# A hybrid attention and recurrence layer: which engine copies the second head's weights, how the recurrence's output is stored, and when the decay column is projected

## The chip, the core and the metric

The kernel runs on one core of a Trainium2 chip. The metric is the device time of one execution in microseconds (us); the time of a kernel is the median over its runs. The engines are PE (matrix products), DVE (VectorE), ACT (ScalarE), POOL (GpSimd) and SP, which here only issues DMA transfers. A measurement of this kernel tells a difference of about 0.2%, some 3.6 us, from no change.

## The reference, cut

One layer over 1024 tokens with 16 meta tokens ahead of them (1040 rows), width 1024. Its input projection feeds two branches; everything is fp32.

```python
xn = rms_norm(h, norm_mix[layer])
proj = xn @ w_in[layer]
q_sb, k_sb, v_sb, rw, gate_sb, gate_rw = jnp.split(proj, in_splits, axis=-1)
# branch 1: stick-breaking attention, 8 heads of 64, causal (s < t), z = q.k / 8
#   A[t,s] = sigmoid(z_ts) * prod_{s<j<t} (1 - sigmoid(z_tj));  y_sb = A @ v
# branch 2: RWKV-7 recurrence, 8 heads of 64
rw = token_shift(rw, mu_rw[layer])
r, kr, vr, w_lo, a_lo, g_lo = jnp.split(rw, rw_splits, axis=-1)
w_log = -jax.nn.softplus(-(w0[layer] + jnp.tanh(w_lo) @ w_up[layer])) - 0.5
decay = jnp.exp(-jnp.exp(w_log))
a = jax.nn.sigmoid(a0[layer] + a_lo @ a_up[layer])
g = jax.nn.sigmoid(g_lo) @ g_up[layer]
# S_t = S_{t-1} diag(decay_t) + (S_{t-1} (-kk_t)) (kk_t * a_t)^T + v_t k_t^T ;  y_t = S_t r_t
y_rw = rwkv7_recurrence(r_h, split_heads(decay, RW_HEADS), k_h, v_h, kk, a_h)
y_rw = (group_norm_heads(y_rw, ...) + bonus) * g
merged = sigmoid(gate_sb) * (y_sb @ w_sb_out) + sigmoid(gate_rw) * (y_rw @ w_rw_out)
h = h + merged @ w_out[layer]
hn = rms_norm(h, norm_ffn[layer])
gate_ffn, up_ffn = jnp.split(hn @ w_ffn_in[layer], [FFN_HIDDEN], axis=-1)
h = h + (jax.nn.silu(gate_ffn) * up_ffn) @ w_ffn_out[layer]
return rms_norm(h, norm_final)[:, N_META:N_META + s]
```

## The kernel before, in words

**Split numbers.** Every fp32 operand of a large product is split into a rounded part "hi" (a copy on ACT, L146 or L155) and the rounded rest "lo" (a subtraction on DVE, L147; for weights on DVE or, where the flag LOP[0] is set, on POOL, L156). A product is then three matmuls: hi by hi, lo by hi, hi by lo (L254 to L256 in the projection).

**Start.** The input is normalised and transposed, and the first column of the input projection starts while that goes on: `wa`, the column of 128 weights that holds the low-rank decay and learning-rate inputs (`win[0]`, L284). A column is 8 k-steps of 3 matmuls over three pieces of 348, 346 and 346 tokens: 72 matmuls. Then `g_cols` (from L590) projects the output gate's two low-rank columns (`win[1]` and the 32-row `wg2`), applies the sigmoid (L606), splits the results (L146, L147, and L611) and multiplies them by the gate's second factor: eight banks `psg` of 512 tokens, four matmuls each (L621 to L624), copied by DVE (L625) and stored as `d_G`.

**Recurrence.** It works in chunks of 64 tokens. A unit is 8 or 9 chunks of one pair of heads; there are 8 units. Three generators (`stage1`, `stage2a`, `stage2b`) make a unit's chunk matrices, solve them, and run the chain of states (`Sbd`, L533 to L538). At the end of a unit `stage2b` transposes its output (L558), scales it on ACT (L560), adds the bonus (L561), multiplies by the gate (L564) and stores it as fp32 in `d_y` (L565, on SP). PE's order is written by a loop that gives every step a time by hand and fills with the remaining projection columns (`sb_col`: attention's q, k, v and the branch gates). Those columns leave through a ring of two tiles named `stage`, stored by POOL's DMA queue. The other engines' order is the framework scheduler's.

**Attention.** Per pair of heads and block i of 128 queries, and per head h: `psz` = q.k (L788, L789, mask L791), two sigmoids on ACT (`ub` L792, `be` L793), a running product over `ub` on DVE (L795), its product with `be` on DVE (L796), transposes of the weights on PE into banks `psaT` of up to four blocks (L804), copies of those banks to `aT`: the first 16 rows by ACT (L807), the rest of a first bank by DVE and later banks by ACT (L809, L810), then `pso` = weights by v for both heads (L814) and a split of that (`ysh`, `ysl`). While attention waits, PE is filled with the recurrent branch's product `psbr` (L836 to L838): its input is loaded from `d_y` in eight pieces `yv` (L825) and split there into `yrh` (ACT, L146) and `yrl` (DVE, L147).

**Behind that** come the attention branch's product, the output projection, the FFN's first product in two halves of seven block products each (L957 to L959), the second product (`psfo`, L1119 to L1121, its tiles in the pool `w5`), and the last norm.

Of the kernel before, what the change touches and what calls it, by code (L numbers as in the profile page):

```python
# [10 lines left out]
F32 = mybir.dt.float32  # L11
F32R = mybir.dt.float32r
BF16 = mybir.dt.bfloat16
AF = mybir.ActivationFunctionType
# [5 lines left out]
S = 1024  # L20
# [74 lines left out]
def _build(nc, tc, I, out, dbg, es):  # L95
# [5 lines left out]
    V, A, G, T, SY = nc.vector, nc.scalar, nc.gpsimd, nc.tensor, nc.sync  # L101
# [37 lines left out]
    d_k = dr.tile([2, 4, 128, L], F32, name="d_k")  # L139
    d_v = dr.tile([4, 128, L], F32, name="d_v")  # L140
    d_g = dr.tile([16, 128, S], F32, name="d_g")
    d_y = dr.tile([4, 128, S], F32, name="d_y")
    d_G = dr.tile([4, 128, S], F32, name="d_G")

    def split(hi, lo, src):
        A.copy(hi, src)  # L146
        V.tensor_tensor(lo, src, hi.bitcast(F32), op=ALU.subtract)  # L147
# [131 lines left out]
    def drain(g):  # L279
        for _ in g:  # L280
            pass

    wa = rp.tile([128, LP], F32, name="wa")
    drain(proj_shift(I["win"][0], 0, wa))  # L284
    A.activation(wa[0:64], wa[0:64], AF.Tanh)

    RW = ((1, "kr"), (0, "r"), (2, "v"))

# [231 lines left out]
    def stage2b(p, u, s1, GM, St):  # L520
# [41 lines left out]
        gt = t2("gt", [128, 512])  # L562
        SY.dma_start(gt, d_G[p, :, 512 * u:512 * u + 512])
        V.tensor_tensor(y, y, gt, op=ALU.mult)  # L564
        SY.dma_start(d_y[p, :, 512 * u:512 * u + 512], y)  # L565
        yield 0.45, 0.0
        return St

# [22 lines left out]
    def g_cols():  # L591
# [19 lines left out]
        A.copy(g3[64:96], t[:, 64:])  # L611
        split(u3_[0:32], u3_[64:96], ur)
        A.copy(u3_[32:64], ur)
        for p in range(4):
            if p % 2 == 0:
                st = rp2.tile([128, 2, S], F32, tag="UB", name="gUB", bufs=2)
            for j in range(2):
                ps = bank(("mm", "A")[j], "psg")
                sl = slice(512 * j, 512 * j + 512)
                pr = slice(128 * p, 128 * p + 128)  # L620
                T.matmul(ps, uh[:, pr], hi[:, sl], start=True, stop=False)  # L621
                T.matmul(ps, uh[:, pr], lo[:, sl], start=False, stop=False)
                T.matmul(ps, ul[:, pr], hi[:, sl], start=False, stop=False)
                T.matmul(ps, u3_[:, pr], g3[:, sl], start=False, stop=True)  # L624
                V.tensor_copy(st[:, p % 2, sl], ps)  # L625
            G.dma_start(d_G[p], st[:, p % 2])
# [100 lines left out]
    with ExitStack() as s2:  # L727
# [15 lines left out]
        for p in range(4):  # L743
# [25 lines left out]
            for i in range(8):  # L769
# [10 lines left out]
                for h in range(2):  # L780
# [18 lines left out]
                    for b0 in range(0, nb, 4):  # L799
                        m = min(nb, b0 + 4) - b0  # L800
                        ps = bank("SB"[(b0 // 4) % 2], "psaT")
                        for b in range(b0, b0 + m):
                            s0_, sn = blk[b]
                            T.transpose(ps[:sn, (b - b0) * 128:(b - b0) * 128 + 128], be[:, s0_:s0_ + sn], ident)  # L804
                        f = 0
                        if b0 == 0:
                            A.copy(aT[:16, 0], ps[:16, 0:128])  # L807
                            f = 1
                        ev = A.copy if b0 // 4 else V.tensor_copy  # L809
                        ev(aT[:, b0 + f:b0 + m], ps[:, f * 128:m * 128].rearrange("p (b x) -> p b x", x=128))  # L810

                for b in range(nb - 1, -1, -1):
# [5 lines left out]
        with ExitStack() as s3:  # L818
# [1 line left out]
            yrh = b3.tile([128, 4, S], F32R, name="yrh")  # L820
            yrl = b3.tile([128, 4, S], F32R, name="yrl")
            for p in range(4):
                for j in range(2):
                    yv = b3.tile([128, 512], F32, tag="gt", name="yv", bufs=2)
                    SY.dma_start(yv, d_y[p, :, 512 * j:512 * j + 512])  # L825
                    split(yrh[:, p, 512 * j:512 * j + 512], yrl[:, p, 512 * j:512 * j + 512], yv)
            for d in range(8):
                hi, lo = wload(I["wbr"][1, d], 512)
                for half in range(2):
# [10 lines left out]
    if "ysb" in dbg:  # L840
        SY.dma_start(dbg["ysb"].rearrange("k p t -> p k t"), ysh.bitcast(F32))
    if "yrw" in dbg:
        SY.dma_start(dbg["yrw"], d_y)


    msA, msB, wos = ExitStack(), ExitStack(), ExitStack()
# [217 lines left out]


    with ExitStack() as s4:
        w5 = pool(s4, "w5")
        ft = lambda nm, bufs, dt=F32: w5.tile([128, 512], dt, tag=nm, name=nm, bufs=bufs)
        wr = {}
        gfin = None  # L1070
# [97 lines left out]
```

## Time and profile before

| | |
|---|---|
| median of 3 runs | 1794.55 us (1793.61 to 1795.46) |
| profiled execution, its own time | 1788.92 us |
| its span in the trace | 1787.2 us |
| PE busy in the span | 1706.4 us, 95% |
| DVE, ACT, POOL busy | 66%, 43%, 22% |
| mean granted clock of PE in 775 to 975 us | 1.00 |

A page's busy shares are means over very different stages, so the table by stretches says more: start and first columns to 55 us, gate products to 77 us, first recurrence columns to 125 us, recurrence to about 625 us, rest of the projection to 775 us, attention with the recurrent branch to 975 us, then attention's branch, output projection and FFN. The granted clock is 1.00 where PE runs at 2.4 GHz and 0.50 where it runs at 1.2 GHz.

### The profile page before, as it was taken

The numbers are of one execution on the slowest core, as the hardware profiler recorded it, in microseconds if no ns is written. First come the engines' busy times: TensorE is split into PE (matmuls) and PEld (weight loads), VectorE is DVE, ScalarE is ACT, GpSimd is POOL, SyncE is SP. The second block draws the span as 40 slices with busy tenths as digits, with TensorE's granted clock in tenths as the row PEclk, the third lists the DMA queues.
The fourth block names the chain that finished last, engine by engine and source line by source line (L and its number), as shares of the span: only waits on it lengthen the run. The fifth ranks groups of instructions, "written<-read, shape, count | busy, mean of one in ns | idle before, by whom it ended". The sixth has DMA issues, their size and how long they took to land.

```text
span 1787.2 us, 28844 instructions
## 1 busy us (share of the span) xinstructions
PE 1706.4 (95%) x11120; PEld 1407.7 (79%) x11120; DVE 1171.1 (66%) x1969; ACT 770.3 (43%) x1542; POOL 387.0 (22%) x393
## 2 busy tenths in 40 slices
PE   7999999999999999998989999999999999999998
PEld 6787888888897788866666887788888888778886
DVE  6345654655655632078988844898887877579756
ACT  7344354444545533256655323532333332254445
POOL 2222112211111221300000001365454544210000
PEclk9999989999999999999999999999999999999999
DMA  5223213211211354225422535133333323297233
GB/s 173 71 77 97 70 49 95 57 54 40 80 41 50 94 127 127 89 74 129 119 72 63 180 129 189 50 116 100 107 118 100 106 89 100 93 323 250 89 107 129
DMA packets 98249, 188.79 MB, mean 106 GB/s; under 512 B 38592, under 2 KB 40912, under 8 KB 98112
## 3 DMA queue, kind: packets, MB, share of 16 engines
q1 hardware_dynamic: 83536, 139.63, 26.5%
q0 software_dynamic: 14576, 47.32, 7.0%
q8 instruction: 88, 1.44, 0.3%
q14 instruction: 49, 0.40, 0.1%
HBM read 133.49 MB, written 53.41 MB: 105 GB/s over the span
## 4 chain that ended last, share of the span: by engine, by line
PE 76%; DVE 12%; ACT 5%; issue 4%; DMA 3%; SPq 1%; POOL 0%; ACTq 0%; DVEq 0%; POOLq 0%
PE psf L959 8%; PE psf L958 8%; PE psm L254 8%; PE psf L957 8%; PE psm L255 7%; PE psm L256 7%; PE psfo L1120 4%; PE psfo L1121 4%; PE psfo L1119 4%; DVE ub L795 3%; DVE be L796 2%; PE psC L530 1%; PE pso L814 1%; PE psaT L804 1%; PE pswo L906 1%
## 5 line engine op out<-in xcount | busy, mean ns | idle before, releaser
L254 PE MATMUL psm<-xhi,whi 128*128 128x346 f32 (+3 forms) x872 | 326.8, 375 | 2.6 <-DVE stagel L147 1.8
L255 PE MATMUL psm<-xlo,whi 128*128 128x346 f32 (+3 forms) x872 | 308.7, 354 | 0.3 <-DVE xlo L147 0.3
L256 PE MATMUL psm<-xhi,wlo 128*128 128x346 f32 (+3 forms) x872 | 308.5, 354 | 0.0
L254 PEld LDWEIGHTS psm<-xhi,whi 128*128 128x128 f32 (+1 forms) x872 | 166.0, 190 | 30.4 <-issue 10.7
L256 PEld LDWEIGHTS psm<-xhi,wlo 128*128 128x128 f32 (+1 forms) x872 | 165.5, 190 | 15.5
L255 PEld LDWEIGHTS psm<-xlo,whi 128*128 128x128 f32 (+1 forms) x872 | 166.2, 191 | 13.8 <-DVE xlo L147 0.7
L156 POOL TENSOR_TENSOR wlo<-wraw,whi 128x1024 fp32r<-128x1024 f32 (+1 forms) x42 | 100.3, 2389 | 290.7 <-ACT whi L155 257.4
L1119 PE MATMUL psfo<-wh,ah 128*128 128x512 f32 x308 | 120.7, 392 | 2.5 <-ACT wh L146 2.5
L1120 PE MATMUL psfo<-wl,ah 128*128 128x512 f32 x308 | 121.0, 393 | 2.2 <-DVE wl L147 2.2
L1121 PE MATMUL psfo<-wh,al 128*128 128x512 f32 x308 | 120.8, 392 | 0.0
L146 ACT CAST sh<-S 128x512 fp32r<-128x512 f32 x88 | 54.5, 622 | 144.5 <-PE psf L958 135.8
L155 ACT CAST whi<-wraw 128x1024 fp32r<-128x1024 f32 (+2 forms) x71 | 67.0, 943 | 96.6 <-PE psm L255 36.0
L795 DVE TENSOR_TENSOR_SCAN ub<-ub 128x144 f32<-128x144 f32 (+7 forms) x64 | 87.7, 1381 | 4.2 <-ACT ub L792 4.2
L1047 DVE TENSOR_TENSOR g<-g,sg 128x512 f32<-128x512 f32 x44 | 78.4, 1781 | 15.5 <-ACT sg L1046 14.0
L146 ACT CAST ah<-ar 128x512 fp32r<-128x512 f32 x77 | 47.9, 622 | 92.5 <-PE psfo L1120 58.7
L147 DVE TENSOR_TENSOR al<-ar,ah 128x512 fp32r<-128x512 f32 x77 | 56.5, 734 | 42.4 <-ACT ah L146 42.3
L156 DVE TENSOR_TENSOR wlo<-wraw,whi 128x512 fp32r<-128x512 f32 (+1 forms) x29 | 28.4, 979 | 74.8 <-ACT whi L155 74.8
L147 DVE TENSOR_TENSOR sl<-S,sh 128x512 fp32r<-128x512 f32 x85 | 74.8, 881 | 0.0
L1119 PEld LDWEIGHTS psfo<-wh,ah 128*128 128x128 f32 x308 | 58.4, 190 | 15.1 <-ACT wh L146 2.9
L1120 PEld LDWEIGHTS psfo<-wl,ah 128*128 128x128 f32 x308 | 58.4, 190 | 14.6 <-DVE wl L147 2.5
L1121 PEld LDWEIGHTS psfo<-wh,al 128*128 128x128 f32 x308 | 58.4, 190 | 12.2
L536 DVE TENSOR_SCALAR Sbd<-psC,gam 64x64 f32<-64x64 f32 x64 | 18.5, 289 | 74.5 <-PE psC L533 73.8
(386 smaller groups left out, 4197.0 us busy)
## 6 DMA issues: line engine op xcount, KB each, us to landing
wr<-in_wffi SPq DMA_DIRECT2D x46, 512.0 KB, 3.6
wraw<-in_win SPq DMA_DIRECT2D x42, 512.0 KB, 3.9
ar<-d_a SPq DMA_DIRECT2D x77, 256.0 KB, 2.8
d_a<-sa POOLq DMA_DIRECT2D x44, 256.0 KB, 2.8
wf<-in_wffo SPq DMA_DIRECT2D x44, 256.0 KB, 5.3
d_a<-sg POOLq DMA_DIRECT2D x33, 256.0 KB, 2.4
d_g<-stage POOLq DMA_DIRECT2D x32, 256.0 KB, 3.1
gt<-d_g SPq DMA_DIRECT2D x32, 256.0 KB, 2.6
```

The costliest lines, as they stand in the source:

```text
L147: V.tensor_tensor(lo, src, hi.bitcast(F32), op=ALU.subtract)
L156: (G if LOP[0] else V).tensor_tensor(lo, raw, hi.bitcast(F32), op=ALU.subtract)
L254: T.matmul(ps[:M, :n], hv[:, k], xhi[:, k, t0:t0 + n], start=(k == 0), stop=False)
L255: T.matmul(ps[:M, :n], hv[:, k], xlo[:, k, t0:t0 + n], start=False, stop=False)
L256: T.matmul(ps[:M, :n], lv[:, k], xhi[:, k, t0:t0 + n], start=False, stop=(k == 7))
L795: V.tensor_tensor_scan(rv, rv, rv, 1.0, op0=ALU.mult, op1=ALU.bypass)
L957: T.matmul(ps, wa_[0][:, kc], xa_[0][:, k], start=(k == 0), stop=False)
L958: T.matmul(ps, wa_[0][:, kc], xa_[1][:, k], start=False, stop=False)
L959: T.matmul(ps, wa_[1][:, kc], xa_[0][:, k], start=False, stop=(k == 3))
L1119: T.matmul(ps, ah[:, tt], wh, start=(i == 0), stop=False)
L1120: T.matmul(ps, ah[:, tt], wl, start=False, stop=False)
L1121: T.matmul(ps, al[:, tt], wh, start=False, stop=(i == NP - 1))
```

## The change

1. The projection of `win[0]` moves from the start into `g_cols`, between the splits of the gate's low-rank results and the `d_G` products. LOP[0] is set there, so its low weights are made by POOL and no longer by DVE; the kernel's first column is now `win[1]`.
2. `stage2b` splits its output itself, into two tiles of the `stage` ring, and stores both parts in `d_y`, which is twice as large.
3. In attention, ACT copies the first bank of weights too, where it is the second head's (h = 1).
4. `yrh` and `yrl` are loaded from `d_y` in eight transfers of 512 KB; the loads `yv` and the split behind them go.
5. The pool `w5` of the last stage lies on the other side of the memory.

```diff
@@ -139,7 +139,7 @@
     d_k = dr.tile([2, 4, 128, L], F32, name="d_k")
     d_v = dr.tile([4, 128, L], F32, name="d_v")
     d_g = dr.tile([16, 128, S], F32, name="d_g")
-    d_y = dr.tile([4, 128, S], F32, name="d_y")
+    d_y = dr.tile([2, 4, 128, S], F32, name="d_y")
     d_G = dr.tile([4, 128, S], F32, name="d_G")
 
     def split(hi, lo, src):
@@ -281,8 +281,6 @@
             pass
 
     wa = rp.tile([128, LP], F32, name="wa")
-    drain(proj_shift(I["win"][0], 0, wa))
-    A.activation(wa[0:64], wa[0:64], AF.Tanh)
 
     RW = ((1, "kr"), (0, "r"), (2, "v"))
 
@@ -562,7 +560,10 @@
         gt = t2("gt", [128, 512])
         SY.dma_start(gt, d_G[p, :, 512 * u:512 * u + 512])
         V.tensor_tensor(y, y, gt, op=ALU.mult)
-        SY.dma_start(d_y[p, :, 512 * u:512 * u + 512], y)
+        st = [rp2.tile([128, 512], F32R, tag="stage", name="y" + x, bufs=2) for x in "hl"]
+        split(st[0], st[1], y)
+        for x in range(2):
+            SY.dma_start(d_y[x, p, :, 512 * u:512 * u + 512], st[x].bitcast(F32))
         yield 0.45, 0.0
         return St
 
@@ -611,6 +612,9 @@
         A.copy(g3[64:96], t[:, 64:])
         split(u3_[0:32], u3_[64:96], ur)
         A.copy(u3_[32:64], ur)
+
+        drain(proj_shift(I["win"][0], 0, wa))
+        A.activation(wa[0:64], wa[0:64], AF.Tanh)
         for p in range(4):
             if p % 2 == 0:
                 st = rp2.tile([128, 2, S], F32, tag="UB", name="gUB", bufs=2)
@@ -806,7 +810,7 @@
                         if b0 == 0:
                             A.copy(aT[:16, 0], ps[:16, 0:128])
                             f = 1
-                        ev = A.copy if b0 // 4 else V.tensor_copy
+                        ev = A.copy if b0 // 4 or h else V.tensor_copy
                         ev(aT[:, b0 + f:b0 + m], ps[:, f * 128:m * 128].rearrange("p (b x) -> p b x", x=128))
 
                 for b in range(nb - 1, -1, -1):
@@ -820,10 +824,8 @@
             yrh = b3.tile([128, 4, S], F32R, name="yrh")
             yrl = b3.tile([128, 4, S], F32R, name="yrl")
             for p in range(4):
-                for j in range(2):
-                    yv = b3.tile([128, 512], F32, tag="gt", name="yv", bufs=2)
-                    SY.dma_start(yv, d_y[p, :, 512 * j:512 * j + 512])
-                    split(yrh[:, p, 512 * j:512 * j + 512], yrl[:, p, 512 * j:512 * j + 512], yv)
+                SY.dma_start(yrh[:, p].bitcast(F32), d_y[0, p])
+                SY.dma_start(yrl[:, p].bitcast(F32), d_y[1, p])
             for d in range(8):
                 hi, lo = wload(I["wbr"][1, d], 512)
                 for half in range(2):
@@ -1064,7 +1066,7 @@
 
 
     with ExitStack() as s4:
-        w5 = pool(s4, "w5")
+        w5 = pool(s4, "w5", side="right")
         ft = lambda nm, bufs, dt=F32: w5.tile([128, 512], dt, tag=nm, name=nm, bufs=bufs)
         wr = {}
         gfin = None
```

PE's order changes at the start and in attention. PE around the `d_G` products before, the end of the first fifteen matmuls and what follows (`gUA` is the 32-row column's split result, `psg` the eight banks):

```order
L621 MATMUL psg_694<-gpr_549,gat_554 128x512
L622 MATMUL psg_694<-gAV_550,gat_554 128x512
L623 MATMUL psg_694<-gpr_549,gcc_555 128x512
L624 MATMUL psg_667<-gUA_656,gsq_657 128x512
L624 MATMUL psg_673<-gUA_656,gsq_657 128x512
L624 MATMUL psg_680<-gUA_656,gsq_657 128x512
L624 MATMUL psg_686<-gUA_656,gsq_657 128x512
L624 MATMUL psg_694<-gUA_656,gsq_657 128x512
L621 MATMUL psg_707<-gpr_549,gat_554 128x512
L622 MATMUL psg_707<-gAV_550,gat_554 128x512
```

The same place with the change:

```order
L256 MATMUL psm_637<-xhi_107,wlo_573 128x346
L625 MATMUL psg_667<-gpr_453,gat_458 128x512
L626 MATMUL psg_667<-gAV_454,gat_458 128x512
L627 MATMUL psg_667<-gpr_453,gcc_459 128x512
L628 MATMUL psg_667<-gUA_560,gsq_561 128x512
L625 MATMUL psg_673<-gpr_453,gat_458 128x512
L626 MATMUL psg_673<-gAV_454,gat_458 128x512
L627 MATMUL psg_673<-gpr_453,gcc_459 128x512
L628 MATMUL psg_673<-gUA_560,gsq_561 128x512
```

Five banks were begun ahead of the product that needs `gUA`; now the 72 matmuls of the moved column stand there, and every bank is done in one go.

ACT at the end of recurrence unit 0 before (`Yt` the unit's output, `TT` the solve's matrix, `sg` and `at` the next unit's decay and rate):

```order
L560 ACTIVATE Yt<-psyT,cvec 128x512
L469 COPY TT<-psU_2413 16x8x16 x2
L325 ACT_TABLE_LOAD
L325 ACTIVATE sg<-psw,cvec 128x5x64
L329 ACTIVATE at<-psa,cvec 128x320
L482 COPY Xs<-psX 32x256
```

And with the change:

```order
L558 ACTIVATE Yt<-psyT,cvec 128x512
L146 CAST yh<-Yt 128x512
L467 COPY TT<-psU_2418 16x8x16 x2
L323 ACT_TABLE_LOAD
L323 ACTIVATE sg<-psw,cvec 128x5x64
L327 ACTIVATE at<-psa,cvec 128x320
L480 COPY Xs<-psX 32x256
```

The copy `yh` stands ahead of the copies of `TT`, which the solve waits for; line numbers are smaller by two.

ACT in attention before, the end of block i = 6 and the start of block 7 of the third pair of heads (`aT00` is the first head's, `aT10` the second's):

```order
L793 ACTIVATE be_9128<-psz_9129 128x348
L807 COPY aT00_7615<-psaT_9067 16x128
L792 ACTIVATE ub_9127<-psz_9134 128x348
L793 ACTIVATE be_9128<-psz_9134 128x348
L792 ACTIVATE ub_9127<-psz_9139 128x344
L793 ACTIVATE be_9128<-psz_9139 128x344
L810 COPY aT10_7617<-psaT_9102 128x512
L807 COPY aT10_7617<-psaT_9095 16x128
L792 ACTIVATE ub_9163<-psz_9165 128x348
L793 ACTIVATE be_9164<-psz_9165 128x348
```

And with the change:

```order
L796 ACTIVATE ub_9167<-psz_9179 128x344
L797 ACTIVATE be_9168<-psz_9179 128x344
L811 COPY aT10_7657<-psaT_9135 16x128
L814 COPY aT10_7657<-psaT_9135 128x384
L814 COPY aT10_7657<-psaT_9142 128x512
L796 ACTIVATE ub_9203<-psz_9205 128x348
L797 ACTIVATE be_9204<-psz_9205 128x348
L796 ACTIVATE ub_9203<-psz_9210 128x348
L797 ACTIVATE be_9204<-psz_9210 128x348
L146 CAST ysh_7672<-pso_9091 128x128
```

The second head's 16-row copy is followed by a copy of 384 columns that DVE made before. ACT's and DVE's order is unchanged behind attention.

## Rows read from the trace of the kernel before

**Rows 1.** The page: busy time, share of the span and instructions of each engine.
```profile
PE 1706.4 (95%) x11120; PEld 1407.7 (79%) x11120; DVE 1171.1 (66%) x1969; ACT 770.3 (43%) x1542; POOL 387.0 (22%) x393
```

**Rows 2.** Windows: start:end, length, busy of PE, PEld, DVE, ACT, POOL; clock, DMA, GB/s.
```profile
55.00:77.00 22.00, 18.37 (x85) 14.44 (x83) 10.73 (x16) 6.51 (x10) 4.99 (x8) 0.84 0.30 111
...
125.00:625.00 500.00, 474.36 (x4459) 410.12 (x4458) 296.08 (x713) 235.13 (x471) 97.35 (x103) 0.97 0.24 68
...
775.00:975.00 200.00, 178.38 (x1468) 131.97 (x1469) 179.62 (x254) 125.38 (x368) 0.00 (x0) 1.00 0.33 85
...
1175.00:1550.00 375.00, 375.00 (x1632) 306.09 (x1631) 301.63 (x355) 114.98 (x175) 186.70 (x165) 1.00 0.31 101
```

**Rows 3.** Timeline around the d_G products: start, duration, engine, line, [idle before <- releaser].
```profile
59.88 0.39 PE L621 MATMUL psg<-gpr,gat 128*128 128x512 f32 x1
...
60.11 0.39 PE L622 MATMUL psg<-gAV,gat 128*128 128x512 f32 x1
...
65.80 1.22 DVE L147 TENSOR_TENSOR gUA<-gpv,gUA 32x1024 fp32r<-32x1024 f32 x1 [2.31 <-ACT gUA L146]
...
67.17 2.47 PE L624 MATMUL psg<-gUA,gsq 96*128 96x512 f32 x5 [3.63 <-DVE gUA L147]
...
73.82 0.39 PE L624 MATMUL psg<-gUA,gsq 96*128 96x512 f32 x1
```

**Rows 4.** Timeline: the first and the first following matmul of a 128-row column.
```profile
37.15 0.32 PE L254 MATMUL psm<-xhi,whi 128*128 128x348 f32 x1
...
48.60 0.32 PE L254 MATMUL psm<-xhi,whi 128*32 128x348 f32 x1
```

**Rows 5.** Timeline at the ends of recurrence units 0, 2 and 1.
```profile
244.55 2.37 POOL L156 TENSOR_TENSOR wlo<-wraw,whi 128x1024 fp32r<-128x1024 f32 x1 [11.70 <-ACT whi L155]
...
245.45 1.49 DVE L274 SCALAR_TENSOR_TENSOR v<-last,cvec,v 128x1 f32<-128x1 f32 x1
...
248.87 0.53 ACT L469 COPY TT<-psU 16x128 f32<-16x128 f32 x2 [2.78 <-DVE TT L469]
...
393.78 0.53 ACT L469 COPY TT<-psU 16x128 f32<-16x128 f32 x2
...
303.13 0.33 SPq L565 DMA_DIRECT2D d_y<-Yt  x1
```

**Rows 6.** Windows: the stretch right behind the end of unit 0.
```profile
248.40:258.90 10.50, 9.06 (x85) 6.16 (x85) 4.72 (x9) 7.80 (x16) 0.77 (x2) 0.60 0.23 82
```

**Rows 7.** Groups by shape, 775 to 975 us: busy, mean ns of one, idle before.
```profile
L810 DVE COPY aT<-psaT 128x384 f32<-128x384 f32 x48 | 26.2, 545 | 4.9 <-ACT aT L807 4.9
...
L147 DVE TENSOR_TENSOR yrl<-yv,yrh 128x512 fp32r<-128x512 f32 x8 | 5.3, 674 | 0.0
...
L146 ACT CAST yrh<-yv 128x512 fp32r<-128x512 f32 x8 | 5.0, 623 | 0.0
...
L810 ACT COPY aT<-psaT 128x384 f32<-128x384 f32 x8 | 3.8, 480 | 1.3 <-PE psaT L804 1.2
```

**Rows 8.** Chain of waits by line, 775 to 975 us, and two of its pieces.
```profile
by line: DVE ub L795 29.9%; DVE be L796 14.2%; PE pso L814 11.4%; PE psaT L804 10.4%; DVE aT L810 6.3%; issue 3.5%; ACT ub L792 3.1%; PE psz L788 2.5%; PE psbr L838 2.1%; PE psz L789 2.0%; PE psbr L837 2.0%; DVE ysl L147 1.8%; PE psbr L836 
...
780.86 0.58 DVE yrl L147
...
807.15 0.60 DVE yrl L147
```

**Rows 9.** Waits, 775 to 975 us: us in total, times, longest us.
```profile
PE psaT L804 <- DVE be L796: 9.4, 13, 1.8
...
PE psz L788 <- ACT be L793: 3.6, 7, 0.7
...
PE pso L814 <- DVE aT L810: 2.3, 5, 0.7
...
PE pso L814 <- DVE ysl L147: 2.1, 5, 0.5
```

**Rows 10.** Timeline at the start of the second FFN product.
```profile
1563.85 0.49 PE L1119 MATMUL psfo<-wh,ah 128*128 128x512 f32 x1 [2.47 <-ACT wh L146]
```

More of the change, by code (lines that the diff above doesn't have):

```diff
@@ L842, in _build @@
     if "yrw" in dbg:
-        SY.dma_start(dbg["yrw"], d_y)
+        SY.dma_start(dbg["yrw"], d_y[0])
     msA, msB, wos = ExitStack(), ExitStack(), ExitStack()
```

## The prediction

> **What bounds the kernel now.** I read the page first: PE is busy 95% of the span, DVE 66% and ACT 43% [rows 1]. So time can only be won where PE waits or runs at half clock. The windows show where that is [rows 2]. From 1175 to 1550 us PE is busy 375.00 of 375 us: the FFN is bound by PE, and whatever is won or lost ahead of it arrives at the end unchanged. In attention, 775 to 975 us, PE idles 21.6 us and DVE is the busiest engine with 179.6 of 200, ACT has 125.4. Around the d_G products, 55 to 77 us, the clock is 0.84. In the recurrence, 125 to 625 us, PE idles 25.6 us, in many small waits. Then I read the timeline where the change cuts in, the groups by shape for durations, and the chain and the waits of attention.
>
> **1. The moved column.** At 59.88 us PE begins fifteen matmuls of five banks, then waits 3.63 us for gUA, which DVE finishes at 65.80 + 1.22 = 67.02 [rows 3]. The five products behind the wait take 2.47 us, and the stage's last matmul starts at 73.82. From 59.88 to 73.82 + 0.23 = 74.05 pass 14.2 us for 32 matmuls. At full clock one follows the other after 60.11 - 59.88 = 0.23 us [rows 3], so 32 need 7.5 us. Waiting and half clock (0.50 behind the wait) thus cost 6.7 us. A 128-row column takes 48.60 - 37.15 = 11.4 us [rows 4], longer than the 7.1 us from 59.88 until gUA is there. Put between, it covers the wait, and the clock has no idle engine ahead of it. Nothing is added: the column's 72 matmuls, its load and its ACT and DVE work are moved. Its weights' low part goes from DVE to POOL (2.37 us for such a one [rows 5]), but the start's first column, now win[1], had its on POOL as well; the load queue of SP changes only in which 512 KB comes first. I put this at nothing, with 1 us either way. Term: **-6.7 us**. Bounds: 0, if an equal wait appears behind the moved column, and -7.7.
>
> **2. The split in the recurrence.** Eight times ACT gets a copy of 128x512 (0.62 us by yrh's row) and DVE a subtraction (0.67 by yrl's) [rows 7]; SP gets one more issue of 0.33 us [rows 5] each, ahead of the gathers for the next solve. This is 5.0 us on ACT, 5.4 on DVE, 2.6 on SP. Who stands behind? On ACT the copy of TT. In unit 0 ACT was idle 2.78 us ahead of it, waiting for DVE, so yh costs nothing there; in unit 2 it runs without any idle [rows 5], and everything behind is 0.6 us later. PE has dense columns to fill with, so most of this is hidden. Where it isn't, the engine behind pays twice, because an idle PE falls to half clock: right behind unit 0 the clock was 0.60 for 10.5 us with 9.06 busy [rows 6]. Bounds: from -1 us (a shifted wait may also end sooner) to 8 x 0.8 = +6 us. I take **+1 us**, nearer the rows that show cover.
>
> **3. The second head's copies.** DVE loses 32 copies: 24 of 384 columns, 545 ns each [rows 7], and eight smaller ones of 128 or 256. On the chain two pieces of DVE work stand some 0.09 us closer than they last (0.58 against 0.67 for yrl, [rows 7, 8]), so the 24 give 24 x 0.46 = 11.0 us; the small ones, scaled by their columns, some 2.4: 13.4 us. ACT pays 24 x 0.48 = 11.5 and likewise 2.5: +14.0.
>
> **4. The loads of y.** DVE loses eight yrl, 8 x 0.58 = 4.7 us, ACT eight yrh, 5.0 us. So ACT goes from 125.4 to about 134 us of 200, and DVE from 179.6 down by 18. SP's eight loads of 256 KB become eight of 512 KB; they wait for no ring any more, so they start as soon as the memory is free.
>
> What of 18 us does PE see? Only what lies on the chain: the aT copies are 6.3% of 200 us there [rows 8], 12.6 us for both heads, so 6.3 for one. Four of the eight yrl are on it (the first and the last are shown), 2.3 us. That is 8.6. From above: PE's waits that end with DVE are 9.4 + 2.3 + 2.1 = 13.8 us [rows 9]; PE can't win more. The waits for ACT's sigmoids, 3.6 us, stay and can grow, since the second head's copies now stand between them. I take **-10 us**, nearer the chain, with 0 and -13.8 as the bounds for the range. What is late next is the running product (29.9% of the chain), which stays on DVE.
>
> Here a rule of the Trainium skill speaks against the change. The row first: the same copy out of PSUM, 128x384 fp32, takes 480 ns on ACT and 545 on DVE [rows 7]. The page "ScalarE: Activation LUTs", section "Rules for kernel authors", says of simple elementwise work to use VectorE, not ScalarE, as VectorE is up to about 3 times faster in bf16. By it 24 copies would cost ACT as much as 24 x 1.6 = 39 us instead of 11.5, an estimate from that page's factor. By the rows the rule does not hold for this copy, and the sum goes by the rows.
>
> **5. The pool on the other side.** At the start of the second FFN product PE waits 2.47 us [rows 10] for ACT's split of the weights, not for memory, and ACT's order is the same. I cost it at **0**; if the old placement delayed the loads, up to 2.5 us would be won.
>
> **The sum.** -6.7 + 1 - 10 + 0 = -15.7 us. The profiled execution took 1788.92 us, so 1773.2 by its count; it lies 5.6 us under the median of 1794.55. On the median: **1778.9 us**.
>
> **Rivals.** (a) ACT becomes attention's bound. For it: ACT rises to 134 us while DVE falls to 162, and ACT handles sigmoids, 16-row copies and the new copies in one queue, waiting for PE's transposes in order. Against: 66 us of slack. If attention yields nothing, 1794.55 - 5.7 = 1788.9. (b) Slower: the end of each recurrence unit stalls the chain of states. yl, with both inputs in SBUF, is held while POOL makes a column's low weights: a DVE operation on a single column took 1.49 us beside POOL's 2.37 us [rows 5]; the Sbd steps queue behind it on DVE, and the two stage tiles stay occupied until their stores land, which stops the projection's columns too. Price: 2.37 + 0.67 = 3.0 us of PE idling per unit, and about as much again as half of it at half clock, 1.5; eight units 36 us, so 1794.55 - 16.7 + 36 = 1813.9. It decides from 16.7 / 8 = 2.1 us per unit on. For it: PE's order is fixed, it can't step aside. Against: POOL is busy 97.4 of 500 us there [rows 2], one time in five. The page "SBUF — State Buffer", section "Who interferes with whom", names that case: a DVE instruction with two SBUF inputs contends with a GpSimd instruction that reads SBUF, and the loser blocks for the whole instruction. The 1.49 us agree with it; the chance goes by POOL's share. (c) The relief arrives in full, 13.8 us, and the loads help as well: 1794.55 - 5.7 - 13.8 - 2.5 = 1772.5. (d) The change doesn't do what it says at the start: the wait for gUA only moves, as the kr column's weights or the d_G copies come late. Then 1794.55 + 1 - 10 = 1785.6.
>
> **Chances.** The forecast, 1774 to 1784: 0.55; (c) 0.17; (d) 0.07; (a) 0.11; (b) or a part of it 0.10. The range leaves out (b)'s far part and a little below (c): 1767 (c with its 5 us of spread below) to 1791. Within 0.2% (3.6 us, what a measurement can tell) of 1794.55 lie the weak part of (b) and the upper edge of (a): 0.09. Slower: 0.07. Faster: 0.84.
>
> **What the profile after would show.** Right at the start: full clock through the d_G products and no wait for gUA. In attention: DVE busy about 162 us, PE's waits for be and aT down by two thirds, ACT near 134. In the recurrence: PE's idle time the same within a few us. I am wrong if ACT's sigmoids take the waits over, if the Sbd steps stand behind yl, or if the clock falls somewhere new.

## The result, and the profile after

The changed kernel takes 1805.76 us (median of 4 runs, 1804.64 to 1808.37), the kernel before 1794.08 us in the same comparison: ratio 1.0073, 95% interval 1.0060 to 1.0085. It is slower, and the forecast of 1778.9 us was 27 us off, with the wrong sign. Of all runs below one, of the kernel with all but the y split, took 2357.07 us in a slow state and is left out of its row.

Where the time went shows when the spans of the two profiled executions are cut at the same four places of PE's program: the last d_G matmul, the first psz of attention, the first matmul of attention's branch, the end.

| stage, us | before | after | difference |
|---|---|---|---|
| start, to the last d_G matmul | 73.8 | 69.6 | -4.2 |
| recurrence, to the first psz | 696.2 | 723.5 | **+27.3** |
| attention, to its branch's product | 215.8 | 211.7 | -4.1 |
| rest | 801.4 | 801.9 | +0.5 |
| of the recurrence, PE at 1.2 GHz | 34.1 | 64.9 | +30.8 |

The two gains of the forecast came, smaller. What swallowed them is the recurrence, where the forecast had +1 us.

The differences add up to 19.5 us, where the medians differ by 11.7: the profiled execution of before (1788.92 us) lies 5.2 us under its median, that of the changed kernel (1808.37 us) 2.6 over. So single stage differences can be a few us too large. Five other kernels below leave the recurrence's own work as it was; there it takes 697.3 to 699.1 us, 1 to 3 more than in this execution of before, and the loss in the recurrence stands at some 25 us against them.

The page, engines:

```profile
PE 1714.2 (95%) x11120; PEld 1415.2 (78%) x11120; DVE 1164.8 (64%) x1936; ACT 779.7 (43%) x1573; POOL 387.9 (21%) x394
```

Against [rows 1] PE has the same instructions and 8 us more busy time, as more of them ran at half clock; the span grew by 19 us, so the rest is idle time.

Windows of after (length; busy of PE, PEld, DVE, ACT, POOL; clock, DMA share, GB/s): the d_G stretch of [rows 2], then the recurrence, the stretch behind unit 1's end, and attention, each by its own bounds:

```profile
55.00:77.00 22.00, 22.00 (x126) 20.63 (x125) 10.22 (x17) 7.23 (x12) 4.86 (x7) 1.00 0.40 144
69.60:793.00 723.40, 681.44 (x5805) 582.36 (x5804) 353.30 (x843) 307.57 (x609) 138.67 (x143) 0.96 0.27 77
...
336.00:352.00 16.00, 12.04 (x197) 10.13 (x199) 4.11 (x11) 2.31 (x6) 0.00 (x0) 0.58 0.09 12
793.00:1004.70 211.70, 192.31 (x1571) 145.03 (x1570) 173.81 (x233) 139.34 (x411) 0.94 (x4) 0.99 0.38 105
```

The d_G stretch is now gapless at clock 1.00 (it was 0.84). The stretch from 336 to 352 us holds one of the two long stays at half clock (338.5 to 352.2 us): clock 0.58 and 4 us idle. For comparison, before: the recurrence by the same bounds, the same piece of program as 336 to 352 us, and attention by the same bounds:

```profile
73.80:770.00 696.20, 670.35 (x5806) 574.16 (x5804) 344.05 (x835) 302.76 (x601) 139.25 (x143) 0.98 0.27 76
336.70:344.80 8.10, 7.14 (x198) 6.15 (x199) 4.11 (x11) 2.21 (x6) 0.00 (x0) 1.00 0.25 72
770.00:985.80 215.80, 193.51 (x1572) 143.64 (x1570) 189.74 (x273) 132.96 (x388) 0.89 (x4) 1.00 0.36 94
```

In the recurrence PE is busy 11.1 us longer with the same matmuls, and idle 42.0 us where it was 25.9: 16.1 us more.

The moved column, first and last matmul of the d_G stage (they answer to [rows 3]):

```profile
62.39 0.39 PE L625 MATMUL psg<-gpr,gat 128*128 128x512 f32 x1
...
69.57 0.39 PE L628 MATMUL psg<-gUA,gsq 96*128 96x512 f32 x1
```

From 62.39 to 69.57 + 0.23 = 69.80 pass 7.4 us for 32 matmuls, where 7.5 were forecast, and no matmul waits for gUA. But the stage began 2.5 us later than its forerunner at 59.88. The delay comes from the first column, now win[1], which waits for its low weights from POOL. Its first matmuls run at half clock (0.49 us apiece and more, where 0.32 is full speed), as those of the first column did before, but until about 24 us and not 22. Its first matmul on the second piece of tokens starts at 29.50 us, before at 26.50:

```profile
18.84 0.66 PE L256 MATMUL psm<-xhi,wlo 128*128 128x348 f32 x1 [0.73 <-POOL wlo L156]
```

PE's waits in the recurrence (us in total, times, longest), after:

```profile
PE psU L453 <- DMA TN<-ds: 7.6, 9, 2.5
PE psU L461 <- DMA TT<-ds: 4.7, 5, 1.6
...
PE psX L478 <- DVE Tn L474: 3.6, 1, 3.6
```

and before:

```profile
PE psU L463 <- DMA TT<-ds: 2.1, 3, 1.0
...
PE psU L455 <- DMA TN<-ds: 1.3, 3, 0.5
```

The new waits are for transfers: TN and TT are the gathers of the solve in stage2a, which goes through DRAM in four hops on SP's queue: UA to zs, zs to Z, the result Tt to ds and back as TN, its transpose Tw to ds and back as TT. SP's queue around the solve behind unit 1, before (start, duration, line, out<-in, count):

```profile
303.51 4.84 SPq L415 DMA_DIRECT2D zs<-UA  x8
...
327.54 0.31 SPq L440 DMA_DIRECT2D ds<-Tt  x1
328.44 0.30 SPq L445 DMA_DIRECT2D ds<-Tw  x1
329.81 3.67 SPq L442 DMA_DIRECT2D TN<-ds  x8
333.58 3.71 SPq L447 DMA_DIRECT2D TT<-ds  x8
337.39 0.38 SPq L152 DMA_DIRECT2D wraw<-in_win  x1
```

and after:

```profile
300.94 0.33 SPq L413 DMA_DIRECT2D zs<-UA  x1
301.77 0.34 SPq L566 DMA_DIRECT2D d_y<-yh  x1
302.50 0.32 SPq L566 DMA_DIRECT2D d_y<-yl  x1
302.86 4.45 SPq L413 DMA_DIRECT2D zs<-UA  x7
...
328.46 0.31 SPq L438 DMA_DIRECT2D ds<-Tt  x1
331.43 0.35 SPq L152 DMA_DIRECT2D wraw<-in_win  x1
331.83 3.99 SPq L440 DMA_DIRECT2D TN<-ds  x8
336.16 0.31 SPq L443 DMA_DIRECT2D ds<-Tw  x1
337.85 4.76 SPq L445 DMA_DIRECT2D TT<-ds  x8
```

Three things differ. The two stores stand among the zs gathers, and wait there for ACT's yh and DVE's yl. A weight load (wraw, 331.43), which waits for POOL to give a buffer back, stands ahead of the TN gathers, where it stood behind TT before. And Tw is stored behind TN, not ahead of it. TT, which ended at 337.29 before, ends at 342.61. From the first zs to the end of TT pass 41.7 us, before 33.8. By these rows, of the 7.9 us more 1.4 lie ahead of Z's load, 2.1 in the solve up to the store of Tt, 1.1 between that store and the first TN, where the weight load now stands, and 3.3 from there to the end of TT, as TT needs Tw. PE, whose order is fixed, waits for both gathers, and runs at half clock from 338.5 to 352.2 us:

```profile
336.42 0.22 PE L453 MATMUL psU<-TN,UA 32*32 32x32 f32 x2 [2.52 <-DMA TN<-ds]
...
343.10 0.41 PE L461 MATMUL psU<-TT,Xq 32*32 32x32 f32 x4 [1.60 <-DMA TT<-ds]
```

The solve itself ends later too. DVE's steps of the solve (L435 and L437, the first two columns of a row are start and duration), before:

```profile
320.06 0.21 DVE L435 TENSOR_TENSOR Tm<-Z,Tt 72x55 f32<-72x55 f32 x1
320.30 0.21 DVE L437 TENSOR_TENSOR Tt<-Tt,Tm 72x55 f32<-72x55 f32 x1
```

after, where they are L433 and L435:

```profile
324.53 0.19 DVE L433 TENSOR_TENSOR Tm<-Z,Tt 72x39 f32<-72x39 f32 x1
324.64 0.68 DVE L362 SCALAR_TENSOR_TENSOR AV<-kkn,E 64x512 f32<-64x512 f32 x1
325.24 0.18 DVE L435 TENSOR_TENSOR Tt<-Tt,Tm 72x39 f32<-72x39 f32 x1
...
329.18 2.47 DVE L442 COPY Tw<-Tt 72x256 f32<-72x256 f32 x1
```

Packed, one follows the other after 0.25 us; where an operation of 0.68 us on 512 columns stands between every two, each takes 0.7 to 0.9 us. Before, the last five operations of the solve are spaced like that, after, the last eight. From Z's load to the store of Tt pass 19.6 us (308.85 to 328.46), before 17.6 (309.99 to 327.54). The copy Tw takes 2.47 us, where 0.37 are normal, beside POOL's operation on the next weights:

```profile
328.83 2.58 POOL L156 TENSOR_TENSOR wlo<-wraw,whi 128x1024 fp32r<-128x1024 f32 x1
```

The Trainium skill has this case: the page "SBUF — State Buffer", section "Who interferes with whom", says that a VectorE copy can take the port pair that it shares with GpSimd, and that whoever issues first holds the pair for its whole instruction while the other blocks. The 2.47 us end 0.24 us behind POOL's 328.83 + 2.58 and agree with it.

Attention, groups by shape and PE's waits (they answer to [rows 7] and [rows 9]):

```profile
L814 ACT COPY aT<-psaT 128x384 f32<-128x384 f32 x32 | 14.8, 466 | 2.2 <-PE psaT L808 2.2
...
L814 DVE COPY aT<-psaT 128x384 f32<-128x384 f32 x24 | 13.2, 550 | 4.5 <-ACT aT L811 4.5
```

```profile
PE psaT L808 <- DVE be L800: 14.4, 18, 2.0
...
PE psz L792 <- ACT be L797: 0.9, 2, 0.5
```

The second head's 24 copies of 384 columns have joined the 8 that ACT had, at 466 ns each. The waits for ACT's sigmoids fell to 0.9 us, from 3.6 in [rows 9] and 3.9 by attention's own bounds; pso's wait for aT (2.3) is gone; but the wait for be, the product behind the running product, rose from 9.4 to 14.4.

The last stage begins, at 1582.87 us, with the same wait of 2.47 us for ACT's wh as in [rows 10].

### The profile page after: what moved, and what is told of

Its sections match the earlier page's. It is cut to its first block, busy times and chain, and to the rows that moved or that the text cites. A ratio compares the mean times of both kernels' runs of the same rounds, so it can differ in the third digit from the quotient of the medians.

```text
span 1806.6 us, 28875 instructions
## 1 busy us (share of the span) xinstructions
PE 1714.2 (95%) x11120; PEld 1415.2 (78%) x11120; DVE 1164.8 (64%) x1936; ACT 779.7 (43%) x1573; POOL 387.9 (21%) x394
## 4 chain that ended last, share of the span: by engine, by line
PE 49%; DVE 8%; issue 2%; ACT 2%; DMA 1%; DVEq 0%; SPq 0%; ACTq 0%
PE psf L961 8%; PE psf L960 8%; PE psf L959 8%; PE psfo L1122 4%; PE psfo L1123 4%; PE psfo L1121 4%; DVE ub L799 3%; DVE be L800 2%; PE pswo L908 2%; PE pswo L907 2%; PE pswo L909 2%; PE psm L254 2%; PE psm L255 1%; PE psm L256 1%; PE psaT L808 1%
## 5 line engine op out<-in xcount | busy, mean ns | idle before, releaser
L254 PE MATMUL psm<-xhi,whi 128*128 128x346 f32 (+4 forms) x872 | 327.8, 376 | 3.1 <-DVE stagel L147 1.8
L256 PE MATMUL psm<-xhi,wlo 128*128 128x346 f32 (+4 forms) x872 | 309.8, 355 | 0.7 <-POOL wlo L156 0.7
L255 PE MATMUL psm<-xlo,whi 128*128 128x346 f32 (+4 forms) x872 | 309.2, 355 | 0.3 <-DVE xlo L147 0.3
L155 ACT CAST whi<-wraw 128x1024 fp32r<-128x1024 f32 (+1 forms) x71 | 66.8, 942 | 94.6 <-PE psm L255 33.5
L808 PE MATMUL psaT<-ident,be 128*128 128x128 f32 (+1 forms) x352 | 55.2, 279 | 16.0 <-DVE be L800 14.4
```

Of the source, the lines that this page charges most:

```text
L254: T.matmul(ps[:M, :n], hv[:, k], xhi[:, k, t0:t0 + n], start=(k == 0), stop=False)
L255: T.matmul(ps[:M, :n], hv[:, k], xlo[:, k, t0:t0 + n], start=False, stop=False)
L256: T.matmul(ps[:M, :n], lv[:, k], xhi[:, k, t0:t0 + n], start=False, stop=(k == 7))
```

## The experiments

Theory A: the loss is made in SP's queue, by the stores of yh and yl and by what the scheduler then moves around them. Theory B: the added copy and subtraction delay the solve on ACT and DVE. A third possibility was that the earlier start alone shifts half-clock stretches to worse places. All stage times are of one profiled execution each; the ratios, to the kernel before in the same comparison, are of 5 to 12 runs.

| kernel | ratio [95%] | median | start | recurrence | attention |
|---|---|---|---|---|---|
| decay column alone (1) | 0.9981 [0.9969, 0.9992] | 1789.06 | 69.1 | 698.8 | 218.1 |
| y split alone (2, 4) | 1.0103 [1.0085, 1.0122] | 1811.77 | 74.0 | 720.7 | 213.8 |
| copies alone (3) | 0.9959 [0.9942, 0.9976] | 1784.55 | 74.7 | 698.4 | 209.2 |
| all but the y split (1, 3, 5) | 0.9933 [0.9913, 0.9953] | 1780.32 | 68.8 | 697.3 | 209.2 |
| split computed, not used | 1.0019 [1.0003, 1.0035] | 1796.91 | 73.1 | 706.5 | 215.8 |
| fp32 y stored twice | 1.0088 [1.0071, 1.0104] | 1810.19 | 73.4 | 715.3 | 218.2 |
| y split alone, stores on POOL | 1.0022 [1.0006, 1.0038] | 1795.44 | 73.7 | 705.8 | 215.1 |
| the change, stores on POOL | 0.9971 [0.9957, 0.9984] | 1789.09 | 68.6 | 702.9 | 210.4 |
| the change, late stores | 0.9991 [0.9976, 1.0005] | 1791.57 | 67.6 | 704.4 | 211.8 |
| parts 1 and 3 alone | 0.9929 [0.9913, 0.9945] | 1780.10 | 68.2 | 697.9 | 209.2 |
| pool side alone (5) | 0.9998 [0.9985, 1.0011] | 1792.24 | 72.3 | 699.1 | 215.8 |
| late stores, no shared ring | 0.9961 [0.9946, 0.9977] | 1785.99 | 68.6 | 704.1 | 213.3 |

Where in the recurrence the time is lost shows when PE's place in the program is compared unit by unit. The table gives how far a kernel is behind before at the first transpose of a unit's output, counted from its last d_G matmul; minus is ahead. Units are counted from 0, two to a pair of heads; behind units 1, 3 and 5 the solves of the next pair go through SP's queue.

| us behind before, at the end of unit | 0 | 1 | 2 | 4 | 6 | 7 |
|---|---|---|---|---|---|---|
| the change | 3.4 | 3.5 | 11.5 | 18.4 | 22.1 | 27.3 |
| y split alone | 2.1 | 0.6 | 7.5 | 14.8 | 20.0 | 24.5 |
| fp32 y stored twice | 0.1 | 0.4 | 7.6 | 14.6 | 19.2 | 19.2 |
| split computed, not used | -0.6 | -0.7 | -2.7 | 1.1 | 2.9 | 10.3 |
| the change, stores on POOL | -0.2 | -0.3 | 1.3 | -0.6 | -0.2 | 6.7 |
| the change, late stores | -1.7 | -1.7 | -1.3 | 1.4 | 1.9 | 8.3 |
| late stores, no shared ring | 1.7 | 1.2 | 3.9 | 5.1 | 8.0 | 8.0 |

So there are two losses. One of 7 to 8 us comes between the ends of units 1 and 2, with some 7 more up to unit 4, wherever a second store of y is on SP ahead of the gathers, with or without the split's work. The other, 4.5 to 7.4 us between the ends of units 6 and 7, comes wherever the split uses the `stage` ring, on whichever queue its stores are.

**The parts one by one.** The decay column alone, the kernel before with two places changed:

```diff
-    drain(proj_shift(I["win"][0], 0, wa))
-    A.activation(wa[0:64], wa[0:64], AF.Tanh)
...
         A.copy(u3_[32:64], ur)
+        drain(proj_shift(I["win"][0], 0, wa))
+        A.activation(wa[0:64], wa[0:64], AF.Tanh)
```

> Only the moved decay column, on the kernel before. Theory (the recurrence's loss comes from the split of y and its stores in SP's queue): the d_G products end 4.1 us earlier as in the changed kernel, and the time is 0 to 4 us under before. Rival (the shift at the start moves the later work so that half-clock stretches get longer; the changed kernel lost 5.2 us at 192 to 206 us before any y was stored): the same long half-clock stretch stands there, about 14 us of clock 0.50, and the time is equal to before or up to 3 us over it.

Measured: the start 4.7 us shorter, the recurrence 2.6 us longer, attention 2.3 us longer (6.8 us of it at half clock, where before had none), in all 0.9981. No half-clock stretch of 14 us came at 192 us; the shift alone does not make the loss. That stretch cost the changed kernel some 5 us ahead of its first store of y. In the other six kernels with the moved column the half clock at that place lasts 6.8 us or less, or is missing, and why it came in this one stays open.

The split alone is the hunks on `d_y`, `stage2b` and the loads of `yrh` and `yrl` from the change:

```diff
-        SY.dma_start(d_y[p, :, 512 * u:512 * u + 512], y)
+        split(st[0], st[1], y)
+        for x in range(2):
+            SY.dma_start(d_y[x, p, :, 512 * u:512 * u + 512], st[x].bitcast(F32))
```

> Only the split of y in the recurrence and the direct loads of yrh and yrl, on the kernel before. Theory: the recurrence is 18 to 24 us longer than before, the solve behind unit 1 waits for its gathers, attention gains 1 to 4 us; in all +15 to +22 us. Rival (the loss is made by the shift at the start): the recurrence is at most 5 us longer, in all 0 to +3 us.

Measured: 1.0103, the recurrence 24.5 us longer, attention 2.0 shorter. This part alone makes the loss, and its recurrence is as long as the changed kernel's within 3 us (720.7 for 723.5).

The copies alone:

```diff
-                        ev = A.copy if b0 // 4 else V.tensor_copy
+                        ev = A.copy if b0 // 4 or h else V.tensor_copy
```

> Only the second head's copies on ACT, on the kernel before. By the prediction's term 3 alone: -5 to -10 us. By what the changed kernel's attention shows (4 us less from the first to the last matmul of the stage, loads of y included): -1 to -4 us. If ACT's queue takes over: 0 or slower.

Measured: 0.9959, more than the changed kernel's attention had suggested: attention is 6.6 us shorter, PE busy 190.7 of 209.2 us there, ACT 142.2. The gain is the forecast's by kind and two thirds of its 10 us, which had the loads of y in it too. The two other kernels with the copies and the old loads have attention at 209.2 us as well.

All but the split of y (the loads yv and their split are back too):

```diff
-        split(st[0], st[1], y)
-        for x in range(2):
-            SY.dma_start(d_y[x, p, :, 512 * u:512 * u + 512], st[x].bitcast(F32))
+        SY.dma_start(d_y[p, :, 512 * u:512 * u + 512], y)
```

> The changed kernel with y stored and split as before (parts 1, 3 and 5 stay). Theory: -5 to -9 us against before, 17 to 21 us under the changed kernel. Rival (the shift at the start): 0 to +3 us against before, the recurrence longer than before although y is stored as before.

Measured: 0.9933, the recurrence 697.3 us, within 1.2 us of before. With the split undone the change gains some 12 us, a little more than was expected.

**What of the split costs.** The split without its stores, and the stores without the split:

```diff
+        st = [rp2.tile([128, 512], F32R, tag="stage", name="y" + x, bufs=2) for x in "hl"]
+        split(st[0], st[1], y)
```

> The kernel before, which in addition computes yh and yl in every unit and does nothing with them; y is stored and loaded as before, SP's order of transfers is the one of before. Theory A (SP's queue: the stores of yh and yl wait there for ACT and DVE, and a weight load comes ahead of the solve's gathers): 0 to +4 us. Theory B (the copy on ACT and the subtraction on DVE delay the solve themselves): +15 to +20 us, the recurrence 20 us longer, like the run with the split alone.

```diff
-        SY.dma_start(d_y[p, :, 512 * u:512 * u + 512], y)
+        for x in range(2):
+            SY.dma_start(d_y[x, p, :, 512 * u:512 * u + 512], y)
```

> The kernel before, which stores its fp32 y twice, in two transfers behind each other on SP, and splits nothing there; it is loaded and split as before. SP's order then has a weight load ahead of the solve's gathers behind units 1 and 5. Theory A: +5 to +15 us, the wait for the gathers behind unit 1 of 2 to 3 us on PE and the half-clock stretch at 340 us come back. Theory B: 0 to +3 us.

Measured: 1.0019 with all of the engines' work and none of the stores (+3.4 us by the medians; its profiled recurrence is 10 us longer, 7.4 of them at the ring behind unit 6, but that execution is 1.6 us over its median and before's is some 5 us under); 1.0088 with one more store a unit and none of the work (+16.7, a little above what was expected). So theory A holds and B falls, for most of it: the second store of a unit costs most of the 19.9 us that the split alone costs. It does so without any wait for yh or yl in the queue. SP's queue in the run with y stored twice, behind unit 1:

```profile
331.15 0.31 SPq L440 DMA_DIRECT2D ds<-Tt  x1
334.12 0.35 SPq L152 DMA_DIRECT2D wraw<-in_win  x1
334.52 0.40 SPq L445 DMA_DIRECT2D ds<-Tw  x1
334.97 4.38 SPq L442 DMA_DIRECT2D TN<-ds  x8
```

The store adds 0.4 us ahead of the gathers, the solve's result comes 3.6 us later than before (331.15 for 327.54), and the weight load stands ahead of Tw and TN again.

The stores moved to POOL's queue:

```diff
-            SY.dma_start(d_y[x, p, :, 512 * u:512 * u + 512], st[x].bitcast(F32))
+            G.dma_start(d_y[x, p, :, 512 * u:512 * u + 512], st[x].bitcast(F32))
```

> The run with the split of y alone, its stores issued by POOL's queue and not SP's; SP's gathers then stand without a store or a weight load among them. Theory A: -2 to +5 us against before, some 15 to 20 us under the split alone. Theory B: +12 to +20 us, as with the stores on SP.

> The changed kernel with the stores of yh and yl issued by POOL's queue. Theory A: about as the run without part 2 and 4 and better by the loads of y, 1776 to 1786 us, faster than before and than the changed kernel. Theory B: 1798 to 1806 us.

Measured: 1.0022 for the split alone (1.0103 with SP), 0.9971 for the whole change (1.0073 with SP; a little slower than expected). The same work and the same bytes, another queue: 0.8% less for the split alone, 1.0% less for the whole change.

**Place, not number.** The stores stay on SP and are as many; behind the odd units they, and the split, are emitted after the next solve's first two hops:

```diff
+        def fin():
+            ...
+        if u == 1 and p < 3:
+            pend.append(fin)
+        else:
+            fin()
...
         SY.dma_start(Tt.rearrange("p t j -> p (t j)"), I["t0"][:npb])
+        while pend:
+            pend.pop(0)()
```

> The changed kernel; behind the odd units (1, 3 and 5) the split of y and its two stores are emitted only after the next solve's first transfers (zs, Z). SP's order then has the eight zs without a store among them and no weight load ahead of the gathers behind units 1 and 3; behind unit 5 the two stores come among the TN gathers. The engines' work is that of the changed kernel. Theory A (place in SP's queue, and what the scheduler makes of it): the late gathers behind units 1 and 3 go, 8 to 14 us under the changed kernel, 1791 to 1798 us; the solve behind unit 5 may still be late. If the number of transfers or the engines' work counts and not the place: 1802 to 1808 us.

Measured: 0.9991, 14 us under the changed kernel by the medians. SP's queue behind unit 1:

```profile
295.79 5.04 SPq L414 DMA_DIRECT2D zs<-UA  x8
...
302.69 0.34 SPq L573 DMA_DIRECT2D d_y<-yh  x1
303.07 0.43 SPq L573 DMA_DIRECT2D d_y<-yl  x1
...
319.69 0.33 SPq L441 DMA_DIRECT2D ds<-Tt  x1
320.58 0.31 SPq L446 DMA_DIRECT2D ds<-Tw  x1
322.16 3.67 SPq L443 DMA_DIRECT2D TN<-ds  x8
325.93 3.71 SPq L448 DMA_DIRECT2D TT<-ds  x8
329.75 0.38 SPq L152 DMA_DIRECT2D wraw<-in_win  x1
```

The eight zs stand alone, the stores behind Z; Tw, TN and TT are in the old order and the weight load is last. From the first zs to the end of TT pass 33.9 us, as before (33.8), where the changed kernel takes 41.7.

**What is left of the engines' work.** In the run with the late stores PE waits 4.2 us for Tn at unit 6, and the run with the split computed alone has the same wait with 3.2 us. DVE there:

```profile
677.09 0.69 DVE L147 TENSOR_TENSOR yl<-Yt,yh 128x512 fp32r<-128x512 f32 x1 [5.00 <-issue]
677.81 0.43 DVE L477 STREAM_TRANSPOSE Tn<-TT 32x256 f32<-32x256 f32 x1
```

DVE stands 5.00 us ahead of yl, and Tn, which the solve waits for, is behind it. yl needs a tile of the `stage` ring. The profile names no releaser for the 5.00 us, but POOL had issued the ring's last store, a branch gate's, at 668.51, and by the trace's landing times it landed at 676.91, 0.18 us ahead of yl:

```profile
668.51 0.54 POOL L600 DMA_DIRECT2D d_g<-stage  x1 [2.63 <-PE psU L456]
```

The test takes the split out of the ring:

```diff
-            st = [rp2.tile([128, 512], F32R, tag="stage", name="y" + x, bufs=2) for x in "hl"]
-            split(st[0], st[1], y)
+            st = [rp2.tile([128, 512], F32R, tag="gt", name="yh"), y.bitcast(F32R)]
+            A.copy(st[0], y)
+            V.tensor_tensor(st[1], y, st[0].bitcast(F32), op=ALU.subtract)
```

> The run with the late stores, its split moreover without the ring that the projection's stores share: yh lies in the tile of the gate factor, which is dead by then, and yl is written over y. So yl waits for no store of POOL's queue. In the run with the late stores, DVE stood 5.0 us ahead of yl at unit 6, PE waited 4.2 us for what is queued behind it, and half clock followed. If that wait is the shared ring: PE's wait for Tn goes, 5 to 8 us under the run with the late stores, 1783 to 1787 us. If it is something else (DVE's own order, the late PE): the wait stays and so does the time, 1790 to 1793 us.

Measured: 0.9961 (late stores with the ring: 0.9991), and PE's wait for Tn is gone. The shared ring cost some 5 us by the runs, at one unit of eight: there the run with the ring falls 6.4 us back against before, this one not at all. The two recurrences in the table, 704.4 and 704.1 us, do not show it, since the profiled execution here is the slowest of its eight and has lost as much in earlier units.

**The rest.** The pool's side alone, and the two parts that gain:

```diff
-        w5 = pool(s4, "w5")
+        w5 = pool(s4, "w5", side="right")
```

> Only the last stage's pool on the other side, on the kernel before. The prediction's 0: within 2 us of before. Rival (the old place delayed the last stage's loads): -2 to -5 us, and the first weight product of that stage starts with less than 2.47 us of waiting.

> The parts 1 and 3 alone, on the kernel before: no split of y, the pool of the last stage where it was. By the runs so far (parts 1, 3 and 5 together took 11 us off): -9 to -12 us, about 1781; if the pool's side (part 5) gave some of that, -6 to -9 us.

Measured: 0.9998 and the same wait of 2.47 us for the pool; 0.9929 for parts 1 and 3 alone, with 1780.10 us as fast as all but the y split, 13 us under before and 26 under the change. The parts do not simply add: -13.3 and +19.9 give +6.6 us, where the change measured +11.7.

## Why the prediction was wrong, point by point

**Step 2, the split in the recurrence, failed.** It priced the extra store as "one more issue of 0.33 us ... each, ahead of the gathers for the next solve", and took +1 us with a bound of 8 x 0.8 = 6. The recurrence grew by 27.3 us in the profiled executions. The sentence named the right neighbours and put the wrong price on them. Its term counts the issue itself, and that is not where the time went: in the run with y stored twice the added store takes 0.4 us of SP's queue and waits for nothing of the split, and the run lost 16.7 us. With the store there, the scheduler's order of DVE and SP behind it came out otherwise. Of the 7.9 us that the chain behind unit 1 got longer in the changed kernel, 2.1 are steps of the serial solve, more of them spaced at 0.7 to 0.9 us and not at 0.25, and 4.4 are the order of SP's queue behind it (the weight load ahead of TN, Tw behind TN); only 1.4 are the stores among the zs. The bound was made from the engines' waits (0.6 us on ACT), and none from the queue's own chain of four hops. The second thing that the term left out is the ring: 5.2 us of the 27.3 come between the ends of units 6 and 7.

**It was in the order of the program.** SP's order with the change shows wraw ahead of TN and Tw behind it, at unit 1. The prediction read the orders of PE, ACT and DVE at three places and took SP's for "which 512 KB comes first" at the start. The one queue whose transfers PE waits for is not in it at the place of the change.

**The clock added to it.** PE's waits for the gathers were 5.4 us behind unit 1 (2.52 + 0.44 + 0.17 + 1.60 + 0.66), but PE fell back by some 10 us there: the same matmul is 3.0 us ahead of before at 326.23 us, and psX is 7.1 behind at 351.63. Of the recurrence's 27.3 us, 16.1 are idle time of PE and 11.1 the same matmuls taking longer, with 30.8 us more at half clock. The prediction had the mechanism ("the engine behind pays twice") and used it for its rival and in a bound of 0.8 us a unit, far too low.

**Rival (b) was the right side for another reason.** It said 1813.9 by yl held beside POOL and by the ring. yl was held by the ring, but at one unit and for 5 us; the gathers were not in it. POOL did hold a DVE operation back, but it was the copy Tw, 2.47 us for 0.37, and its late store is one of the pieces behind unit 1. The rival's chance of 0.10 was set by POOL's share of busy time, which says nothing of where such a hold falls.

**Step 1, -6.7 us, was mis-sized.** The d_G products ran as worked out, 7.4 us. The start gained 4.2 us in the changed kernel, 4.7 with the part alone, and 4.9 as the mean of the seven kernels with the moved column against the seven without. The missing part lies ahead: "the start's first column ... had its on POOL as well" does not hold, since before, the first column's low weights came from DVE in 1.23 us, and now come from POOL in 2.36. PE waits for them (0.73 us) and stays at half clock for longer; the second piece of tokens starts 2.2 us later by the same means. With the part alone the time at the end fell by 2.9 us only, since the recurrence and attention gave some back.

**Steps 3 and 4, -10 us, were mis-sized.** The copies alone gave 6.6 us in attention, the loads with the split alone 2.0; 8.6 together, as the chain's pieces counted (6.3 + 2.3), before 10 were chosen. In the changed kernel both gave only 4.1. ACT did not become the bound: its waits shrank. What is left is the chain through be, the product behind the running product: PE's wait for it is 9.4 us before, 10.6 to 10.9 in the three kernels with the copies and the old loads (attention 209.2 us each), and 14.4 in all four with the copies and the direct loads (210.4 to 213.3 us). So the direct loads, which gain 2.0 us by themselves, lost 1 to 4 us behind the copies, where the term had a gain. One of the four has no half clock in attention, the other three 3.4 to 6.8 us of it. Why be comes later with the direct loads was not tried.

**The price of a copy on ACT held.** 480 ns was taken, 466 measured over 32 copies; DVE's take 550. The Trainium skill's row that gives relu, max, min, add and mul to VectorE, with a factor for bf16 ("ScalarE: Activation LUTs", "Rules for kernel authors"), does not carry over to this fp32 copy. The Trainium skill's page "VectorE: DVE Perf Modes", section "The TRN2 errata", does: its cycles for a source in PSUM give 463 ns on ScalarE and 525 on VectorE for 384 columns, an estimate from its table; the trace agrees within 5%.

**Step 5, the pool, was right:** 0.9998, the same 2.47 us.

What stays open: why the scheduler's order comes out so, and how PE's 10 us behind unit 1 divide between the weight load ahead of the gathers, the late Tw and the spread-out steps of the solve. The cut of the 7.9 us above is read from one trace; every run that moved the stores moved all of these, and none was made that moves one.

## What to carry to other kernels

In this kernel a transfer added to a queue cost what it did to the chain behind it, not its own issue: find the longest chain of dependent transfers on that queue, and try such a store on another queue or behind the gathers. A ring of buffers that a change shares with other stores is a second place to look. Where a scheduler orders the queues, compare the order of every engine and queue at the place of the change, above all of the queue whose landings the fixed engine waits for. And when a change has several parts, time each alone: here two parts gained 13 us together, and the split of y lost 20.

## What the runs showed of the hardware

A store of 256 KB from POOL's queue took 8.4 us to land (issued 668.51, landed 676.91, in the run with the late stores), where such stores of the branch gates land in 3.3 us by the median of that run; around it SP streamed attention's loads. Before, the same store takes 7.3 us, and there no split waits for its tile. No run isolates the cause.

Half-clock stretches changed from kernel to kernel where the program is the same: the changed kernel ran 192 to 205 us at 1.2 GHz, the one with the decay column alone did not, though PE's waits from 175 to 193 us are not far apart (2.6 us and 1.8). Some of the differences of 2 to 4 us between stage times in the table are of this kind, so that small gains need the runs, not one trace.
